# A hybrid S5 and gated DeltaNet block on one core: masks by selection, factored S5 tables, weight splits on VectorE, other figures in the planner of TensorE's order, an earlier first weight tile and five banks for the first transposes

## The chip, the cores and the metric

The kernel runs on one core of one Trainium2 chip. Time is device time in microseconds (us) of the slowest core, here the only one, and the median of three runs is given. Engines are named as in the profile: PE (TensorE), DVE (VectorE), ACT (ScalarE), POOL (GpSimd) and SP (SyncE, which here only issues transfers).

## The reference

One layer, 1024 tokens, 1024 channels, all float32. One projection of the normed input feeds two groups: a diagonal state-space group (S5, 32 groups of 16 channels, 64 states) and a gated DeltaNet group (4 heads of 128). A gate from per-token embeddings and a last norm follow.

In short:

```python
a = rms_norm(h, norm_mix_g[i])
proj = a @ w_in[i]                       # u_s, z_s, q, k, v, z_d, b_raw, a_raw
...
_, _, s_r, s_i = lax.associative_scan(_complex_linear_combine, (a_r, a_i, bu_r, bu_i), axis=1)
y = C_re s_r - C_im s_i + D * u_s; y = gelu(y); y_s = y * sigmoid(y @ w_glu + b_glu) * silu(z_s)
...
qkv = silu(causal_depthwise_conv(qkv, conv_w))          # 4 taps; q, k are L2-normed
g = -exp(A_log) * softplus(a_raw + dt_bias);  beta = sigmoid(b_raw)
g = cumsum(g) in chunks of 64;  decay = tril(exp(g_i - g_j))
sol = triangular_solve(tril(k_beta k^T * decay, -1) + I, [v_beta, k_beta * exp(g)])
per chunk: v_new = u - w S;  o = (q exp(g)) S + (q k^T * decay) v_new;  S = S exp(g_last) + k_dec^T v_new
y_d = rms_norm(o, norm_g) * silu(z_d)
h = h + concat(y_s, y_d) @ w_out
h = h + sigmoid(h @ w_gate) * rms_norm(p @ w_ple_proj, ple_norm_g)
return rms_norm(h, final_norm_g)
```

## The kernel before

**Products.** Float32 products are made of three (`mm3`, L117): each factor is split into a high part in the rounded type fp32r and the rest (`split`, L157: ACT writes the high part, another engine subtracts), and PE multiplies high by high, high by low and low by high. A weight tile (`wtile`, L581) is 128 input channels by 8 blocks of 128: one DMA into the only raw buffer (`wr`), an ACT copy into `wh`, a subtraction into `wl`, both with two buffers. The subtraction is on POOL, but for the tiles named in `EARLY` (L579), where VectorE makes it. `half` (L589) then makes one half of a tile's projection as 24 products of 128x512 into a bank named `pj`, 48 a tile.

**The start.** SP loads the embeddings and their weights, x in eight tiles, constants (`pk`, `wba`), then S5's small parameters (`hp`, and `ldt` in descriptors of single numbers), then the weight tiles, the first of which is number 20 of `win`. `e_proj` (L258) computes the embedding's projection meanwhile and its results are stored to `ed`. VectorE norms the tokens (`rms`, L193), and `scale_x` (L297) scales the eight x tiles. `xprep` (L287) transposes four x blocks into one bank `xtp`, from which ACT makes `ah` and VectorE `al`, the high and low parts of the normed input; eight blocks for the first half of the tokens (hf=0), eight for the second. `MM`, `MX` and `MZ` (L75 to L86) are pools of PE's banks with two or three banks each.

**The prefix scan of `a_raw`.** The decay logits are computed in an exact order of additions: `a_chain` (L1333) runs 64 steps; step n belongs to a group of eight, b = n // 8, and tells one half of the tokens, hf = b % 2. Each step has a part `a_prefix` (L696: three products of a bank `pT` with the masks `tg`; ACT moves it to a buffer F; VectorE subtracts neighbours; ACT makes two more columns) and, two steps on, `a_sums` (L717: four products with the masks `dg`, an ACT copy, four VectorE scans over F). In even groups an ACT copy takes the last column of the scans into `vst` (L730); in odd groups VectorE subtracts the last two columns into `se` (L728). Four buffers F go round. The masks `dg` and `tg`, one pair for each b, are made by `diag` (L327) as four POOL products for a group. The bank `pT` comes from the pool `MX`.

**S5.** `s5_params` (L354) makes the small coefficients and the powers `en` of the rotation by repeated squaring. For each of four batches `s5_batch` (L461) builds a table `tab` of 128 rotations by seven doublings of four POOL operations each (L514 to L525), scans, and puts the results out.

**The gates, the solve and the chunks.** `g_math` (L737) turns the sums in `se` into `gg`; PE transposes it (`gtp`), `decay` (L959) makes the masks, `subst` (L983) solves the 32 blocks on the diagonal, which needs VectorE's columns `cols`; `blocks` (L1045) and `double` (L1057) combine them on PE (`q`); `chunk` (L1171) then runs over the eight pairs of chunks, and `chunk_out` (L1226) norms and gates the result.

**The order.** PE's order is written by hand, by a planner at the end of the program (L1297 to L1469). It keeps a clock that counts only PE's work (`pec`, L104). Chains (`x_chain`, `a_chain`, `s5_chain`, `attn_chain`) yield the figure, from the table `LAT` (L449) or `PL` (L1321), that their next step has to wait; while no chain is due, PE is given the next piece of `fillers` (L1395): the projections in the order of the string `FILL`, then the rows of the glu gate (`pg`), the first half of the output projection (`out1`, L1126), and behind the chunks the rest (`out2`, `htrans`, `gate_out`, L1250). Larger figures so place more filler products ahead of a step. Other engines' orders come from the framework's scheduler, which goes by the program's order and by the inputs; every engine takes its queue in order.

Of the kernel before, what the change touches and what calls it, by code (L numbers as in the profile page):

```python
# [25 lines left out]
def hymba_block_kernel(ctx: ExitStack, tc: tile.TileContext, A: dict, out: bass.AP, dbg=None):  # L26
# [434 lines left out]
    def s5_batch(b):  # L461
# [54 lines left out]
        V.memset(tab[:, 0, :, 0:1], 1.0)  # L516
# [1007 lines left out]
```

## Time and profile before

| | us |
|---|---|
| median of the runs | 955.9 |
| the three runs | 954.72, 955.9, 956.91 |
| the profiled execution | 957.75 |
| its span | 956.0 |
| PE busy | 805.2 (84%) |
| weight loads busy | 649.1 (68%) |
| DVE busy | 709.2 (74%) |
| ACT busy | 489.6 (51%) |
| POOL busy | 343.4 (36%) |

The mean clock that PE was granted in that execution is 0.916 of full speed. The page's picture of the span in 40 equal slices (23.9 us each) shows the busy share of each engine in tenths, 9 for 90% or more, and PE's granted clock in the same way.

```profile
PE   6479889877798976988998597599579999899996
DVE  6946968988999878877548859953778754437886
ACT  7457667676696577766555244112355224113332
POOL 0120458676449348522102022101545219502222
PEclk9779989999899898998999798879789999999998
```

PE is nearly full in the last 170 us, and has slices of 40% and 50% at the start and near 520, 570 and 620 us, which the prediction looks at one by one. In rows of the timeline the first number is the start, the second the duration, and brackets give the idle time of the engine ahead of the instruction and what ended it.

### The profile page before, as it was taken

How to read it: one execution, taken by the hardware profiler on the slowest of the kernel's cores; microseconds unless marked ns; L12 is line 12 of the kernel's file. 1: busy time of each engine (PE TensorE's matmuls, PEld its weight loads, DVE VectorE, ACT ScalarE, POOL GpSimd, SP SyncE). 2: the span in 40 equal slices, each digit the busy share in tenths (PEclk: the TensorE clock that was granted, in tenths of full speed). 3: DMA queues.
4: the chain of work that ended last, by engine and by line, in shares of the span. 5: the costliest groups of instructions: out<-in, count | busy, mean ns of one | idle time of the engine just before them, and what ended most of it. 6: DMA issues, size and time to landing. Idle time of an engine off the chain costs nothing.

```text
span 956.0 us, 12315 instructions
## 1 busy us (share of the span) xinstructions
PE 805.2 (84%) x4338; PEld 649.1 (68%) x4338; DVE 709.2 (74%) x1478; ACT 489.6 (51%) x890; POOL 343.4 (36%) x326
## 2 busy tenths in 40 slices
PE   6479889877798976988998597599579999899996
PEld 3358468756686764876876376488467887778885
DVE  6946968988999878877548859953778754437886
ACT  7457667676696577766555244112355224113332
POOL 0120458676449348522102022101545219502222
PEclk9779989999899898998999798879789999999998
DMA  7430211403122031132102032104445534301211
GB/s 273 154 120 1 88 34 40 110 14 96 37 60 82 34 88 51 23 136 86 66 1 67 22 133 93 40 2 146 108 107 165 194 140 138 129 1 67 88 45 67
DMA packets 67581, 79.93 MB, mean 84 GB/s; under 512 B 23456, under 2 KB 49344, under 8 KB 67520
## 3 DMA queue, kind: packets, MB, share of 16 engines
q1 hardware_dynamic: 67376, 78.89, 25.9%
q8 instruction: 34, 0.56, 0.2%
q14 instruction: 27, 0.22, 0.1%
q10 hardware_dynamic: 144, 0.26, 0.1%
HBM read 57.39 MB, written 21.74 MB: 83 GB/s over the span
## 4 chain that ended last, share of the span: by engine, by line
PE 48%; DVE 27%; ACT 11%; issue 5%; DMA 5%; POOL 4%; SPq 1%; DVEq 0%; ACTq 0%; POOLq 0%
PE pj L111 16%; DVE F L726 9%; PE pq L111 9%; PE pT L111 6%; PE po L111 5%; ACT F L102 5%; DVE s5x L91 3%; PE bk L111 2%; DMA wr<-in_win 2%; DVE cv L99 2%; PE pg L111 2%; DVE pT L91 2%; ACT L102 1%; POOL wgl L91 1%; DVE s5x L554 1%
## 5 line engine op out<-in xcount | busy, mean ns | idle before, releaser
L111 PE MATMUL pj<-ah,wh 128*128 128x512 f32 x384 | 161.8, 421 | 12.3 <-ACT z L102 6.0
L111 PE MATMUL pj<-ah,wl 128*128 128x512 f32 x384 | 156.8, 408 | 0.7 <-POOL wl L91 0.7
L111 PE MATMUL pj<-al,wh 128*128 128x512 f32 x384 | 157.3, 410 | 0.0
L102 ACT ACTIVATE F<-F,gridc 128x512 f32<-128x512 f32 x128 | 115.2, 986 | 0.0
L91 POOL TENSOR_TENSOR wl<-wr,wh 128x1024 fp32r<-128x1024 f32 x21 | 52.2, 2485 | 137.6 <-ACT wh L102 137.6
L111 PEld LDWEIGHTS pj<-ah,wh 128*128 128x128 f32 x384 | 76.7, 200 | 31.9 <-ACT z L102 6.4
L111 PE MATMUL pT<-tg,ah 128*128 128x512 f32 x128 | 58.0, 453 | 47.0 <-ACT F L102 45.6
L726 DVE TENSOR_TENSOR_SCAN F<-F,vst 128x192 f32<-128x192 f32 x128 | 92.9, 784 | 3.2 <-ACT F L102 3.1
L726 DVE TENSOR_TENSOR_SCAN F<-F 128x192 f32<-128x192 f32 x128 | 85.7, 729 | 7.2 <-ACT F L102 7.1
L111 PEld LDWEIGHTS pj<-ah,wl 128*128 128x128 f32 x384 | 75.9, 198 | 19.5 <-POOL wl L91 1.2
L111 PEld LDWEIGHTS pj<-al,wh 128*128 128x128 f32 x384 | 76.4, 199 | 16.4
L91 DVE TENSOR_TENSOR pT<-F 128x512 f32<-128x512 f32 x64 | 51.0, 797 | 47.9 <-ACT F L102 46.4
L111 PEld LDWEIGHTS pT<-tg,ah 128*128 128x128 f32 x128 | 26.3, 205 | 60.7 <-ACT F L102 51.1
L111 PE MATMUL pq<-wgl,hth 128*128 128x512 f32 (+1 forms) x200 | 66.9, 386 | 0.0
L102 ACT ACTIVATE F<-pT 128x512 f32<-128x512 f32 x64 | 55.5, 867 | 2.1 <-PE pT L111 2.1
L99 DVE SCALAR_TENSOR_TENSOR cv<-raw,pk,cv 128x1023 f32<-128x1023 f32 (+2 forms) x36 | 52.9, 1470 | 3.9 <-ACT cv L102 3.8
L91 POOL TENSOR_TENSOR e<-e,pleg 128x1024 f32<-128x1024 f32 x8 | 19.3, 2412 | 97.7 <-ACT jq L102 88.3
L91 DVE TENSOR_TENSOR h<-h,po 128x512 f32<-128x512 f32 x32 | 21.9, 686 | 40.9 <-PE po L111 40.8
L102 ACT ACTIVATE F<-pT,tbl 128x128 f32<-128x128 f32 x128 | 36.5, 372 | 28.4 <-PE pT L111 28.3
L706 POOL COPY F<-tbl 128x4 f32<-128x4 f32 x32 | 16.5, 517 | 84.5 <-DVE pT L91 84.5
L102 ACT ACTIVATE wh<-wr 128x1024 fp32r<-128x1024 f32 x24 | 25.3, 1052 | 37.9 <-DMA wr<-in_win 14.9
L111 PE MATMUL pT<-dg,al 128*128 128x512 f32 x128 | 44.2, 429 | 0.0
(337 smaller groups left out, 2033.5 us busy)
## 6 DMA issues: line engine op xcount, KB each, us to landing
wr<-in_win SPq DMA_DIRECT2D x24, 512.0 KB, 3.7
x<-in_x SPq DMA_DIRECT2D x8, 512.0 KB, 8.1
wr<-in_wout SPq DMA_DIRECT2D x8, 512.0 KB, 4.0
h<-in_x SPq DMA_DIRECT2D x8, 512.0 KB, 4.6
wr<-in_wgate SPq DMA_DIRECT2D x8, 512.0 KB, 3.3
e<-ed SPq DMA_DIRECT2D x8, 512.0 KB, 3.2
out<-h SPq DMA_DIRECT2D x7, 512.0 KB, 2.6
ed<-e SPq DMA_DIRECT2D x6, 512.0 KB, 12.6
```

Of the source, the lines that this page charges most:

```text
L91: return e.tensor_tensor(out=o, in0=a, in1=b, op=op)
L99: return e.scalar_tensor_tensor(out=o, in0=a, scalar=s, in1=b, op0=op0, op1=op1)
L102: return S.activation(out=o, in_=i, func=f, **k)
L111: return PE.matmul(o, lhsT=l, rhs=r, start=a, stop=z, **k)
L554: V.tensor_tensor_scan(out=flat(w[:, ri]), data0=flat(rh), data1=flat(v[:, ri]), initial=0.0, op0=MUL, op1=ADD)
L706: G.tensor_copy(out=tb[:, :, 0:1], in_=first)
L726: V.tensor_tensor_scan(out=d0, data0=d0, data1=d1, initial=vst[:, i, h:h + 1] if hf else 0.0, op0=ADD, op1=ADD)
```

## The change

- **First weights:** the DMA of weight tile 20 is issued right behind `wba`, ahead of S5's `hp` and `ldt`, and `wtile` takes it from there.
- **Banks at the start:** `e_proj` and the first half's `xprep` take two of five banks from `MX`, the others from their old pool; `x_chain` yields 0 in the first half, where it yielded 1.2.
- **x:** `scale_x` is one tile at a time; tiles 0 to 3 are scaled as before, tiles 4 to 7 between the first four `xprep`. The split of weight tile 21 is held until tile 0 is scaled.
- **Splits:** every weight tile's `wl` is subtracted on VectorE; the list `EARLY` goes.
- **Selections:** the masks of a group are two `affine_select`s on POOL of 128x1024 instead of four products of 128x512.
- **Tables:** `s5_params` builds two small tables once for all batches (16 and 8 rotations, in the new tile `rt4`, by `rotate`, four and three doublings of four POOL operations), and `s5_batch` makes `tab` as their product: eight POOL products of 2x8x16 elements and two operations of 512.
- **`se`:** odd groups copy the last two columns on ACT into `se2`, as even groups copy `vst`; one subtraction in `g_math` makes `se` of them, in a buffer F.
- **Planner:** six figures in `LAT` and three in `PL`.
- **Smaller:** `rr`, `v2` and `tq` of `chunk` live in `rt4`; the scratch tiles of `rsqrt` with 32 columns and more have one buffer.

```diff
-        p = MM("pe")
+        p = (MX if i % 5 % 2 else MM)("pe")
...
+    wfirst = {20: raw_w([P, 8, P])}
+    SP.dma_start(out=wfirst[20], in_=A["win"][20].rearrange("p (k c) -> p k c", k=8))
...
-        p = MZ("xtp", [P, 4, P])
+        p = (MX if hf == 0 and k % 5 % 2 else MZ)("xtp", [P, 4, P])
...
-    def scale_x():
-        for i in range(8):
-            r = ts(V, xt_[i], xt_[i], rinvs[:, i:i + 1], MUL)
-        return r
+    sx = {}
+
+    def scale_x(i):
+        sx[i] = ts(V, xt_[i], xt_[i], rinvs[:, i:i + 1], MUL)
...
-    scale_x()
+    for i in range(4):
+        scale_x(i)
...
-    se = C("se", [P, 4, 8, 4])
+    se2 = C("se2", [P, 4, 8, 4, 2])
...
+    wap = C("wap", [P, 8, 2, 4], F32R)
+    V.tensor_copy(out=wap[:, :, 0], in_=wba[:, :, 4:8])
+    tt(V, wap[:, :, 1], wba[:, :, 4:8], wap[:, :, 0].bitcast(F32), SUB)
...
-        for x, w in enumerate((wah.bitcast(F32), wal)):
-            for o, m in zip(res, (ident, tri)):
-                tt(G, o[:, x], w[:, b, :].unsqueeze(2).to_broadcast(sh), m.unsqueeze(1).to_broadcast(sh), MUL)
+        w = wap[:, b].rearrange("p x h -> p (x h)").unsqueeze(2).to_broadcast([P, 8, P])
+        for o, c in zip(res, (ALU.is_equal, ALU.is_ge)):
+            G.affine_select(out=o.rearrange("p x h c -> p (x h) c"), in_=w, pattern=[[0, 8], [1, P]],
+                            compare_op=c, fill=0.0, base=0, channel_multiplier=-1)
...
+    rt4 = C("rt4", [P, 8, P])
+    rtf = rt4.rearrange("p a b -> p (a b)")
+    tbs = [rtf[:, a:z].rearrange("p (r j n) -> p r j n", r=2, j=16) for a, z in ((0, 512), (512, 768))]
+    tbx = rtf[:, 768:1024].rearrange("p (r j n) -> p r j n", r=2, j=16)
+
+    def rotate(tb, x, i, c, s):
+        n = 1 << i
+        tt(G, tb[:, :, :, n:2 * n], tb[:, :, :, 0:n], c, MUL)
+        tt(G, x[:, :, :, 0:n], tb[:, :, :, 0:n], s, MUL)
+        tt(G, tb[:, 0, :, n:2 * n], tb[:, 0, :, n:2 * n], x[:, 1, :, 0:n], SUB)
+        tt(G, tb[:, 1, :, n:2 * n], tb[:, 1, :, n:2 * n], x[:, 0, :, 0:n], ADD)
...
+        for tb, e0, n in ((tbs[0], 0, 4), (tbs[1], 4, 3)):
+            V.memset(tb[:, 0, :, 0:1], 1.0)
+            V.memset(tb[:, 1, :, 0:1], 0.0)
+            for i in range(n):
+                c0, s0 = (e.unsqueeze(1).unsqueeze(3).to_broadcast([P, 2, 16, 1 << i]) for e in en[e0 + i])
+                rotate(tb, tbx, i, c0, s0)
...
-        prep=14.1, ev=3.3, scan=18.0, tab=8.7, g1=13.5, g2=10.6, dec=14.8, sub=14.7, blk=0.3,
-        q32=6.9, d32=6.5, q64=2.0, d64=0.8, kq=4.3, A=1.4, B=4.8, C=1.4, otp=10.3, vtp=23.2, ssq=30.3,
+        prep=14.1, ev=3.3, scan=18.0, tab=6.0, g1=23.0, g2=4.0, dec=14.8, sub=25.0, blk=0.3,
+        q32=6.9, d32=8.0, q64=2.0, d64=0.8, kq=4.3, A=1.4, B=4.8, C=1.4, otp=10.3, vtp=23.2, ssq=30.3,
...
-        V.memset(tab[:, 0, :, 0:1], 1.0)
-        V.memset(tab[:, 1, :, 0:1], 0.0)
-        for i in range(7):
-            n = 1 << i
-            cc = en[i][0][:, pp].unsqueeze(1).unsqueeze(3).to_broadcast([P, 2, 4, n])
-            ss = en[i][1][:, pp].unsqueeze(1).unsqueeze(3).to_broadcast([P, 2, 4, n])
-            tt(G, tab[:, :, :, n:2 * n], tab[:, :, :, 0:n], cc, MUL)
-            tt(G, tb[:, :, :, 0:n], tab[:, :, :, 0:n], ss, MUL)
-            tt(G, tab[:, 0, :, n:2 * n], tab[:, 0, :, n:2 * n], tb[:, 1, :, 0:n], SUB)
-            tt(G, tab[:, 1, :, n:2 * n], tab[:, 1, :, n:2 * n], tb[:, 0, :, 0:n], ADD)
+        t5, x5 = (t.rearrange("p r j (m n) -> p (r j) m n", n=16) for t in (tab, tb))
+        for j in range(4):
+            lo = tbs[0][:, :, 4 * b + j].unsqueeze(2).to_broadcast([P, 2, 8, 16])
+            ch, sh_ = (tbs[1][:, r, 4 * b + j].unsqueeze(1).unsqueeze(3).to_broadcast([P, 2, 8, 16]) for r in range(2))
+            tt(G, t5[:, j:8:4], lo, ch, MUL)
+            tt(G, x5[:, j:8:4], lo, sh_, MUL)
+        tt(G, tab[:, 0], tab[:, 0], tb[:, 1], SUB)
+        tt(G, tab[:, 1], tab[:, 1], tb[:, 0], ADD)
...
-    EARLY = (12, 13, 16)
-
...
-        raw = raw_w([P, 8, P])
-        SP.dma_start(out=raw, in_=A["win"][mt].rearrange("p (k c) -> p k c", k=8))
-        split(hi, lo, raw, S, V if mt in EARLY else G)
+        raw = wfirst.pop(mt, None)
+        if raw is None:
+            raw = raw_w([P, 8, P])
+            SP.dma_start(out=raw, in_=A["win"][mt].rearrange("p (k c) -> p k c", k=8))
+        with ExitStack() as st:
+            if mt == 21:
+                gate(st, sx[0])
+            split(hi, lo, raw, S, V)
...
-            tt(V, se[:, b // 2, i, :], f[:, 382:1536:384], f[:, 383:1536:384], SUB)
+            act(se2[:, b // 2, i], f[:, 0:1536].rearrange("p (h c) -> p h c", h=4)[:, :, 382:384], AF.Copy)
...
+        se = FT[0][:, 0:128].rearrange("p (a b c) -> p a b c", a=4, b=8)
+        tt(V, se, se2[:, :, :, :, 0], se2[:, :, :, :, 1], SUB)
...
-        f0=8.0, x1=26.0, a0=23.9, ca=5.2, s0=34.0, x0=16.7,
+        f0=8.0, x1=20.5, a0=20.5, ca=5.2, s0=30.0, x0=16.7,
...
-            yield LAT["xp"]
+            if hf == 0 and k < 4:
+                scale_x(4 + k)
+            yield LAT["xp"] if hf else 0
```

SP's queue at the start, behind the eight loads of x; `ed<-e` stores the embedding's projection, `wr<-in_win` loads a weight tile. Before:

```order
L281 DMA pk<-in_pk 128x134
L282 DMA wba<-in_wba 128x64
L340 DMA hb_413<-in_hp 128x8
L343 DMA ldt<-in_ldt 64x16x1 x2
L585 DMA wr<-in_win 128x1024
L274 DMA ed<-e 128x1024 x5
L268 DMA ed<-e 128x512
L585 DMA wr<-in_win 128x1024
L268 DMA ed<-e 128x512 x3
```

With the change:

```order
L281 DMA pk<-in_pk 128x134
L282 DMA wba<-in_wba 128x64
L284 DMA wr<-in_win 128x1024
L343 DMA hb_410<-in_hp 128x8
L346 DMA ldt<-in_ldt 64x16x1 x2
L274 DMA ed<-e 128x1024 x5
L268 DMA ed<-e 128x512 x2
L603 DMA wr<-in_win 128x1024
L268 DMA ed<-e 128x512 x2
```

The first weight tile stands ahead of `hp` and `ldt`; the second, behind five stores of 128x1024 and one of 128x512 before, now stands behind five and two.

ACT's queue in the last steps of an odd group (F and its number are the four buffers that go round, `raw`, `cv` and `z` evacuate projections, `wh` is the split of a weight tile). Before:

```order
L102 ACTIVATE F_406<-pT,tbl 128x128 x4
L102 ACTIVATE F_408<-pT 128x512
L102 ACTIVATE F_406<-F_406,gridc 128x512 x2
L102 ACTIVATE raw<-pj 128x512
L102 ACTIVATE cv<-pj,pk 128x512
L102 ACTIVATE F_407<-pT,tbl 128x128 x4
L102 ACTIVATE F_405<-pT 128x512
L102 ACTIVATE F_407<-F_407,gridc 128x512 x2
L102 ACTIVATE wh<-wr 128x1024
L102 ACTIVATE raw<-pj 128x512
L102 ACTIVATE cv<-pj,pk 128x512
```

With the change, where `se_399` is the tile `se2`:

```order
L102 ACTIVATE se_399<-F_403 128x8
L102 ACTIVATE F_406<-pT,tbl 128x128 x4
L102 ACTIVATE F_404<-pT 128x512
L102 ACTIVATE F_406<-F_406,gridc 128x512 x2
L102 ACTIVATE raw<-pj 128x512
L102 ACTIVATE cv<-pj,pk 128x512
L102 ACTIVATE se_399<-F_404 128x8
L102 ACTIVATE F_403<-pT,tbl 128x128 x4
L102 ACTIVATE F_405<-pT 128x512
L102 ACTIVATE F_403<-F_403,gridc 128x512 x2
```

Each odd step now has one copy that reads F behind the scans, and the moves of `pT` to F of later steps stand behind it in the queue.

PE's queue around the first products `q` of the solve (`pj` is a projection, `kq` the attention scores of k and q, `pg` the glu gate). Before:

```order
L111 MATMUL pj<-ah_139,wh 128x512
L111 MATMUL pj<-al_147,wh 128x512
L111 MATMUL pj<-ah_139,wl 128x512
L111 MATMUL q_4656<-q_4289,zt_3646 32x32 x16
L111 MATMUL q_4656<-q_4289,zt_3691 32x32 x16
L111 MATMUL q_4691<-q_4289,zt_3704 32x32 x16
L111 MATMUL q_4691<-q_4289,zt_3739 32x32 x16
L111 MATMUL kq<-q_4289,k_3640 128x128 x4
L111 MATMUL pj<-ah_140,wh 128x512
L111 MATMUL pj<-al_148,wh 128x512
```

With the change:

```order
L111 MATMUL pj<-al_152,wh 128x512
L111 MATMUL pj<-ah_144,wl 128x512
L111 MATMUL kq<-em_4331,k_3516 128x128 x4
L111 MATMUL kq<-q_4345,k_3518 128x128 x8
L111 MATMUL q_4702<-q_4345,zt_3524 32x32 x16
L111 MATMUL q_4702<-q_4345,zt_3537 32x32 x16
L111 MATMUL q_4737<-q_4345,zt_3570 32x32 x16
L111 MATMUL q_4737<-q_4345,zt_3583 32x32 x16
L111 MATMUL kq<-q_4359,k_3520 128x128 x4
L111 MATMUL pg<-gh_4796,wgh 128x512
L111 MATMUL pg<-gl_4795,wgh 128x512
```

The `q` products stood among projections of the fillers; now the last projection is ahead of them, with eight more `kq`, and the glu gate's products follow. Counted from PE's first instruction, 1071 projection products stood ahead of the first `q` before, and all 1152 do now. Between the last `pT` product of the prefix scan and `gtp` the queue had 54 projection products and has 144; between `gtp` and the transposes `pe` that follow, it had 48 and has 18.

In chunk 6 and the front of chunk 7 PE's queue holds no products of the output projection between those of the chunk itself; before, both had them.

More of the change, by code (lines that the diff above doesn't have):

```diff
@@ L130, in rsqrt @@
         n = "rs" + "x".join(map(str, shp[1:]))
-        hb = dp.tile(shp, I32, tag=n + "h", name="hb")
-        t = dp.tile(shp, F32, tag=n + "t", name="rt")
+        hb = dp.tile(shp, I32, tag=n + "h", name="hb", bufs=3 if shp[1] < 32 else 1)
+        t = dp.tile(shp, F32, tag=n + "t", name="rt", bufs=3 if shp[1] < 32 else 1)
         V.tensor_scalar(out=hb, in0=x.bitcast(I32), scalar1=1, scalar2=None, op0=ALU.logical_shift_right)
@@ L322, in hymba_block_kernel @@
     FT = [fp.tile([P, FW], F32, tag="F", name=f"F{i}") for i in range(4)]
-    wah, wal = C("wah", [P, 8, 4], F32R), C("wal", [P, 8, 4])
-    V.tensor_copy(out=wah, in_=wba[:, :, 4:8])
-    tt(V, wal, wba[:, :, 4:8], wah.bitcast(F32), SUB)
+    wap = C("wap", [P, 8, 2, 4], F32R)
+    V.tensor_copy(out=wap[:, :, 0], in_=wba[:, :, 4:8])
+    tt(V, wap[:, :, 1], wba[:, :, 4:8], wap[:, :, 0].bitcast(F32), SUB)
     def diag(b):
-        sh = [P, 4, P]
         res = [T(f"{n}{b}", F32R, [P, 2, 4, P]) for n in ("dg", "tg")]
-        for x, w in enumerate((wah.bitcast(F32), wal)):
-            for o, m in zip(res, (ident, tri)):
-                tt(G, o[:, x], w[:, b, :].unsqueeze(2).to_broadcast(sh), m.unsqueeze(1).to_broadcast(sh), MUL)
+        w = wap[:, b].rearrange("p x h -> p (x h)").unsqueeze(2).to_broadcast([P, 8, P])
+        for o, c in zip(res, (ALU.is_equal, ALU.is_ge)):
+            G.affine_select(out=o.rearrange("p x h c -> p (x h) c"), in_=w, pattern=[[0, 8], [1, P]],
+                            compare_op=c, fill=0.0, base=0, channel_multiplier=-1)
         return res
@@ L1191, in chunk @@
                 mm(bk[:, 2, :], ksl(qq, n, h), Sst[h])
-                rr = dp.tile([P, P], F32, tag="rr", name="rr", bufs=4)
+                rr = rt4[:, h]
                 stt(V, rr, bk[:, 0, :], neg[:, ucs[h]], vr[c][:, i, h, :], MUL, ADD)
-                tq = dp.tile([P, P], F32, tag="tq", name="tq", bufs=4)
+                tq = rt4[:, 4 + h]
                 act(tq, bk[:, 2, :], AF.Copy, scale=eg[:, ucs[h]])
@@ L1202, in chunk @@
             mm(bks[h][:, 1, :], zu(4 * n + h), rrs[h])
-            v2 = rrs[h] if n else dp.tile([P, P], F32, tag="rr", name="v2", bufs=4)
+            v2 = rrs[h] if n else rt4[:, h]
             ts(V, v2, bks[h][:, 1, :], dd[:, ucs[h]], MUL)
```

## Prediction

> **What bounds the kernel now.** I read the stretch table first, cut where the kind of work changes. Columns: busy time (instructions) of PE, weight loads, DVE, ACT, POOL, then the granted clock, DMA share and GB/s.
>
> ```profile
> 0.00:67.00 67.00, 40.02 (x140) 27.96 (x140) 46.43 (x93) 39.01 (x47) 8.70 (x14) 0.86 0.55 195
> 67.00:520.00 453.00, 392.03 (x2012) 312.30 (x2012) 364.88 (x586) 309.56 (x542) 214.50 (x248) 0.93 0.20 58
> 520.00:622.00 102.00, 72.22 (x317) 57.29 (x319) 83.86 (x211) 31.14 (x45) 17.06 (x10) 0.85 0.21 73
> 622.00:786.00 164.00, 143.90 (x1146) 122.58 (x1143) 107.56 (x285) 55.09 (x136) 49.22 (x29) 0.90 0.40 123
> 786.00:956.00 170.00, 157.06 (x733) 128.97 (x732) 106.49 (x306) 54.83 (x122) 53.93 (x26) 0.97 0.22 78
> ```
>
> PE's idle time is what can be won: 27 us before the first prefix product, 61 in the prefix-scan stage (to 520), 30 in the gate chain (to 622), 20 among the chunks, 13 behind them. The wait table (total, times, longest) names the largest cause.
>
> ```profile
> PE pT L111 <- ACT F L102: 45.6, 17, 6.9
> ACT vst L102 <- DVE F L726: 55.7, 21, 5.3
> ```
>
> The scan stage loses PE time through ACT, which itself stands behind VectorE's scans. The gate chain (rows further down) loses it because the planned PE order reaches gtp and q before VectorE has their input.
>
> **The start.** Timeline rows (start, duration; in brackets the idle time before).
>
> ```profile
> ldt<-in_ldt SPq DMA_DIRECT2D x2, 4.0 KB, 18.5
> 20.00:31.00 11.00, 7.39 (x28) 4.48 (x27) 10.89 (x16) 10.87 (x10) 0.00 (x0) 1.00 0.07 4
> 31.00:40.00 9.00, 1.60 (x6) 0.97 (x6) 7.94 (x39) 0.00 (x0) 0.00 (x0) 0.86 0.33 120
> 40.00:50.00 10.00, 7.08 (x21) 5.67 (x22) 8.79 (x17) 3.67 (x6) 2.70 (x1) 0.61 0.84 324
> 41.32 1.06 ACT L102 ACTIVATE wh<-wr 128x1024 fp32r<-128x1024 f32 x1 [10.45 <-DMA wr<-in_win]
> 41.52 7.51 DVE L95 TENSOR_SCALAR x<-x,rsc 128x1024 f32<-128x1024 f32 x8
> 53.72 1.26 ACT L102 ACTIVATE ah<-xtp,pk 128x512 fp32r<-128x512 f32 x2
> 62.76 2.08 PE L115 MATMUL xtp<-cm,x 128*128 128x128 f32 x8 [0.66 <-DVE al L99]
> 69.13 0.80 PE L111 MATMUL pT<-tg,ah 128*128 128x512 f32 x1 [0.78 <-POOL tg L91]
> ```
>
> The first weight tile queues behind ldt, 4 KB that take 18.5 us while the queue moves 4 GB/s, and holds ACT 10.45 us. Ahead of ldt it costs nothing there. What is late next? VectorE finishes the norm at 41.5 as before, plus one split put into it (1.2), then scales four x tiles instead of eight: 3.75, so 46.5. But SP now queues the second weight tile behind seven stores of e (3.07 MB), and ACT and VectorE split it ahead of the first ah and of x4 to x7. About 1.08 MB of the 3.6 move by 40 (9 us at 120 GB/s), the rest needs 2.5 MB / 324 GB/s = 7.7 us: it lands near 48, so the first ah runs at 49 instead of 53.72, minus 4.7. The banks save some 2 us more over the eight pairs (the 0.6 to 2 us waits on al); POOL's two selects come behind the last first-half transpose as its four products did. **Start: minus 7**, from minus 2 (tile at 52) to minus 10 (tile no obstacle).
>
> **The scan stage.** VectorE and POOL first.
>
> ```profile
> L91 POOL TENSOR_TENSOR wl<-wr,wh 128x1024 fp32r<-128x1024 f32 x21 | 52.2, 2485 | 137.6 <-ACT wh L102 137.6
> L91 DVE TENSOR_TENSOR wl<-wr,wh 128x1024 fp32r<-128x1024 f32 x3 | 3.6, 1216 | 10.1 <-ACT wh L102 10.1
> L91 DVE TENSOR_TENSOR se<-F 128x4 f32<-128x4 f32 x32 | 10.5, 328 | 0.5
> L726 DVE TENSOR_TENSOR_SCAN F<-F,vst 128x192 f32<-128x192 f32 x128 | 92.9, 784 | 3.2 <-ACT F L102 3.1
> L726 DVE TENSOR_TENSOR_SCAN F<-F 128x192 f32<-128x192 f32 x128 | 85.7, 729 | 7.2 <-ACT F L102 7.1
> 231.94 1.90 DVE L726 TENSOR_TENSOR_SCAN F<-F 128x192 f32<-128x192 f32 x4
> 238.00 4.00 DVE L726 TENSOR_TENSOR_SCAN F<-F 128x192 f32<-128x192 f32 x4
> 237.49 3.65 POOL L91 TENSOR_TENSOR s5x<-s5x,s5x 128x512 f32<-128x512 f32 x2 [5.01 <-DVE ssq L882]
> 248.76 0.55 DVE L726 TENSOR_TENSOR_SCAN F<-F 128x192 f32<-128x192 f32 x1
> 67.00:520.00 453.00, 20.06 (x32) 67.41 (x112) 0.93 0.20 58
> 67.00:520.00 453.00, 77.04 (x256) 53.39 (x256) 19.15 (x15) 0.93 0.20 58
> L970 POOL TENSOR_SCALAR_AFFINE_SELECT em<-em 128x1024 f32<-128x1024 f32 x3 | 5.0, 1678 | 28.8 <-DVE em L91 28.8
> ```
>
> Four scans take 1.90 us with POOL quiet and 4.00 beside a POOL product; against 0.55 for one alone the two groups carry 128 x 0.234 + 128 x 0.179 = 53 us of excess, 0.25 us for each of POOL's 214.5 in this stage. The GPSIMD Engine Reference of the Trainium skill (Key points) says that GpSimd shares its SBUF interfaces with VectorE and contends with instructions that have two SBUF inputs; the trace agrees, 4.00 against 1.90. By the same rule the moved splits, which read two SBUF inputs, would be stretched too; that is a rival below.
>
> The two stretch rows are those of the table's tile (VectorE's work, then POOL's x112) and of the mask dg (PE, weight loads, then POOL's x15; tg has as much); the last row is an affine select. POOL loses 15 splits (15 x 2.485 = 37). Per batch the tables become eight products of 256 columns and two of 512; at the 1.83 us that one 512-wide product takes above (3.65 for two), and half of that for 256, that is 11 a batch or 44, and 28 small operations once, which the 112 small and large ones put below 0.6 each, 15: 59 for 67. The masks become 14 selects at 1.68, 24 for 38. In all minus 60, so minus 15 of scan excess. VectorE gains 15 x 1.216 = 18 and gives up 10.5 with se. Net minus 7. VectorE is busy in 81% of this stage's 453 us, so I count **minus 6**.
>
> What ACT does in return is the dangerous part.
>
> ```profile
> 252.73 0.21 ACT L102 ACTIVATE vst<-F 128x4 f32<-128x4 f32 x1 [6.11 <-DVE s5tab L516]
> 254.78 0.79 PE L111 MATMUL pT<-tg,ah 128*128 128x512 f32 x1 [6.01 <-ACT F L102]
> ```
>
> A copy of 0.21 us waits 6.11 for VectorE's scans (the row names the memset that stands right behind them); behind it in ACT's queue stand the evacuations that free PE's bank, and PE stands 6.01. So far only the even groups of eight steps have such a copy (vst); the odd ones took se on VectorE, free of any wait on ACT. Now every step has one. Ends for the stage: plus 25 (half of what even steps lose, 45.6, on the odd ones too), and minus 30 (POOL's relief halves the 45.6, VectorE's 7 on top). I take minus 6, nearest to the VectorE rows.
>
> **The gate chain.**
>
> ```profile
> 547.59 0.19 DVE L91 TENSOR_TENSOR gg<-F 128x32 f32<-128x32 f32 x1
> 547.84 0.40 PE L115 MATMUL gtp<-cm,gg 128*32 128x128 f32 x1 [10.78 <-DVE gg L91]
> 550.94 0.21 DVE L849 COPY F<-gls 32x128 f32<-32x128 f32 x1
> 561.50 0.49 PE L115 MATMUL pe<-cm,F 32*128 32x32 f32 x5
> 561.11 1.23 DVE L91 TENSOR_TENSOR wl<-wr,wh 128x1024 fp32r<-128x1024 f32 x1 [9.96 <-ACT wh L102]
> 621.57 3.63 PE L111 MATMUL q<-q,zt 32*32 32x32 f32 x128 [10.70 <-DVE q L1048]
> 507.10 4.19 PE pj L111 x18
> 760.99 1.79 PE bk L111 x16
> 774.88 1.78 PE bk L111 x16
> 683.82 0.80 PE L111 MATMUL pg<-gh,wgh 128*128 128x512 f32 x1 [4.09 <-ACT gh L102]
> ```
>
> A projection product costs 4.19 / 18 = 0.233 us. PE now has 144 of them between the last prefix and gtp where it had 54: 90 x 0.233 = 21 more than the 10.78 that it stands there, so gtp comes up to 10 later than gg, less what VectorE's g_math slips meanwhile: the last v tiles' convolutions now fall ahead of gtp, not behind it. I take 2 late. Between gtp and pe stand 18 products, before 48: VectorE's last row is ready at 551.15, PE reached pe at 561.50, and would now at 552.4: minus 9. **To the first q: minus 7.** Ends: 0 (VectorE stands at wl until ACT's split comes, 9.96 here, so cols is no earlier) and minus 12.
>
> **Behind q.** PE reaches q with 1152 projections done, before 1071: 81 x 0.233 = 18.9 us of work that no longer follows. The 4.09 before pg and the waits like it go (its inputs load while PE waits for q): minus 6. Against it stands a new empty place: the order has no filler in chunk 6 and the front of chunk 7, where out1 is used up and out2 has not begun. A chunk takes 13.9 us (760.99 to 774.88), 39 x 0.233 = 9.1 of them filler. If its chain needs all of that time, the 1.4 chunks idle 13 us, if only PE limits it, none; I take 7. **Minus 18**, ends minus 6 (13 idle) and minus 25 (none).
>
> What else moves I cost at nothing. e's products over five banks: they end under VectorE's norm, which closes at 41.5 whatever PE does; without that cover PE's 27 idle us of the start would move with them. rr and tq in one tile: the same eight blocks of a chunk. The smaller rsqrt buffers: nothing waits for them in these rows.
>
> **The sum.** The profiled execution took 957.75 us, span 956.0; the median of the runs is 955.9, and I carry the difference over to it: 955.9 - 7 - 6 - 7 - 18 = **918**.
>
> **The rivals.**
> - *The copies hold the scans up.* The odd steps lose on ACT what the even ones lose now, 45.6 us, and POOL's relief is used up by the splits: 955.9 - 7 - 7 - 18 + 45.6 = 970, slower. It decides from 32 us on, 1.0 us in each of the 32 odd steps. For it: vst waits 55.7 us in 21 of 32 steps with the same neighbours in the queue. Against it: the wait exists because scans run at 4.00 and not at 1.90, and POOL has 60 us less to disturb them with.
> - *The stage gets all the relief.* Minus 30 there: 894. For it: 45.6 us of PE waiting in 17 places, behind contended scans; against it, VectorE's work hardly falls.
> - *The time is given back later.* Gate chain 0, behind q minus 6: 955.9 - 7 - 6 - 6 = 937. For it: the unfilled chunks, and VectorE's 9.96 in front of cols; against it: PE is 97% granted and over 90% busy from 786 on, so work done before q is work saved.
> - *The splits meet POOL.* POOL stays busy in some 154 of the 453 us, a third; a third of the splits' 18 us would take twice as long, as the scans do: stage 0, 955.9 - 32 = 924. For it the two scan rows, against it the three splits that VectorE does already, mean 1.216 with no stretch to see. (The GPSIMD Engine Reference of the Trainium skill, Key points, gives the ground for it.)
> - *The early load does nothing*, since the second tile holds what the first one held (it lands at 52 or later): start 0, 955.9 - 31 = 925.
>
> **Chances.** Forecast 0.36, full relief 0.20, given back 0.18, splits 0.06, second tile 0.06, coupling 0.14, of which 0.03 end within 0.2% (about what a measurement of this kernel can tell from no change) and 0.11 slower. Faster 0.86. The range goes from 892, just under the full relief's 894, to 948, beyond the given-back case and half way into the coupling; about 0.15 is left out.
>
> **What would show it.** Start: ACT's first split has no wait for wr, the first ah at 49, the first prefix complete near 62; wrong if ACT waits for the second wr beyond 50. Stage: POOL's busy time down by about 60, the mean scan near 0.65 us, the last scan group near 507; wrong if ACT's waits for scans (vst and se2 together) exceed 90 us and PE's wait on ACT grows from 45.6. Gate chain: gtp without a wait, pe within 6 us of it, the first q near 602. Behind it: pg among the d products, one idle place of 5 to 10 us before the last chunk. The prediction falls if the stage from the first prefix to the last scan takes over 480 us.

## The result, and the profile after

The changed kernel takes 929.12 us (median of 4 runs, 927.48 to 930.28) where the kernel before takes 955.72; the ratio is 0.972, with a 95% interval of 0.9701 to 0.9739. The forecast was 918 in a range of 892 to 948: the sign was right, and 27 us came of the 38. The profiled execution took 930.28 us, with a span of 928.6.

| us from the start | before | after | forecast |
|---|---|---|---|
| first `ah` | 53.7 | 49.3 | 49 |
| first prefix product complete | 69.9 | 61.7 | 62 |
| last group of scans ends | 523.8 | 517.4 | 507 (by the terms of its sum 511) |
| `gtp` starts | 547.8 | 552.2 | gg + 2 |
| first `q` | 621.6 | 621.8 | 602 |
| from there to the end | 334.4 | 306.8 | 316 |

So the kernel is 8 us ahead after the start, 6 after the scans, nothing at the first `q`, and 27 at the end. The stretch table of after has the columns of the first one of before (busy time of PE, weight loads, DVE, ACT, POOL, then granted clock, DMA share, GB/s), with the same cuts.

```profile
0.00:67.00 67.00, 41.62 (x168) 31.89 (x169) 47.84 (x97) 41.44 (x52) 4.07 (x13) 0.90 0.54 195
67.00:520.00 453.00, 396.93 (x2039) 313.50 (x2038) 355.93 (x583) 313.20 (x574) 141.98 (x171) 0.93 0.19 58
520.00:622.00 102.00, 75.25 (x353) 60.04 (x353) 85.08 (x197) 36.13 (x48) 20.67 (x12) 0.90 0.36 112
622.00:786.00 164.00, 147.10 (x1176) 126.77 (x1173) 115.21 (x309) 60.02 (x149) 55.22 (x32) 0.92 0.41 126
786.00:928.60 142.60, 129.84 (x613) 106.91 (x611) 94.01 (x281) 41.94 (x103) 33.82 (x17) 0.96 0.16 60
```

POOL fell by 73 us in the scan stage (the forecast had about 60), VectorE by 9, and PE's idle time there only from 61 to 56. The two stretches from the first `q` to the end, before and after, have the same columns.

```profile
621.60:956.00 334.40, 301.36 (x1885) 251.95 (x1885) 214.43 (x592) 110.30 (x259) 103.15 (x55) 0.93 0.31 100
```

```profile
621.80:928.60 306.80, 277.13 (x1788) 233.87 (x1788) 209.41 (x590) 102.16 (x251) 89.04 (x49) 0.94 0.29 95
```

Behind the first `q` PE's busy time fell by 24.2 and its idle time by 3.4: the gain that is left at the end lies there. The wait table of after shows what replaced the old waits.

```profile
ACT vst L102 <- DVE F L747: 50.0, 21, 5.6
...
ACT se L102 <- DVE F L747: 42.4, 23, 5.7
...
PE pT L111 <- ACT F L102: 28.9, 22, 4.5
...
PE q L111 <- DVE q L1071: 20.3, 1, 20.3
```

PE's wait on ACT fell from 45.6 to 28.9, although ACT now waits 92 us for scans (50.0 and 42.4), and PE's wait for `q` doubled to 20.3. The start, in rows of the timeline:

```profile
31.04 1.14 ACT L102 ACTIVATE wh<-wr 128x1024 fp32r<-128x1024 f32 x1
...
48.38 1.06 ACT L102 ACTIVATE wh<-wr 128x1024 fp32r<-128x1024 f32 x1 [10.73 <-DMA wr<-in_win]
49.34 2.40 ACT L102 ACTIVATE ah<-xtp,pk 128x512 fp32r<-128x512 f32 x4
```

```profile
60.75 0.50 PE L111 MATMUL pT<-tg,ah 128*128 128x512 f32 x1 [1.24 <-POOL tg L334]
```

The first split runs at 31.04 without a wait; the second tile holds ACT until 48.38, and the first `ah` follows at 49.34.

### The profile page after: what moved, and what is told of

Read it like the earlier page. It is cut to its first block, busy times and chain, and to the rows that moved or that the text cites. A ratio compares the mean times of both kernels' runs of the same rounds, so it can differ in the third digit from the quotient of the medians.

```text
span 928.6 us, 12239 instructions
## 1 busy us (share of the span) xinstructions
PE 790.8 (85%) x4338; PEld 639.1 (69%) x4338; DVE 698.1 (75%) x1464; ACT 492.7 (53%) x922; POOL 255.8 (28%) x245
## 4 chain that ended last, share of the span: by engine, by line
PE 44%; DVE 30%; ACT 12%; DMA 5%; issue 4%; SPq 2%; POOL 2%; DVEq 0%; ACTq 0%; POOLq 0%
PE pj L111 12%; PE pq L111 10%; DVE F L747 8%; PE po L111 7%; ACT F L102 5%; PE pT L111 5%; PE bk L111 3%; DVE s5x L91 3%; DVE q L91 2%; PE pg L111 2%; DVE pT L91 2%; DVE sq L188 2%; ACT L102 2%; DVE cv L99 2%; DVE xt L91 1%
## 5 line engine op out<-in xcount | busy, mean ns | idle before, releaser
L111 PE MATMUL pj<-ah,wh 128*128 128x512 f32 x384 | 159.5, 415 | 15.2 <-DVE ssq L905 8.6
L111 PE MATMUL pj<-al,wh 128*128 128x512 f32 x384 | 155.1, 404 | 0.0
L747 DVE TENSOR_TENSOR_SCAN F<-F 128x192 f32<-128x192 f32 x128 | 79.8, 681 | 14.6 <-ACT F L102 14.5
L111 PEld LDWEIGHTS pj<-al,wh 128*128 128x128 f32 x384 | 75.5, 197 | 16.3
L747 DVE TENSOR_TENSOR_SCAN F<-F,vst 128x192 f32<-128x192 f32 x128 | 80.0, 686 | 8.0 <-ACT F L102 7.7
L111 PE MATMUL pT<-tg,ah 128*128 128x512 f32 x128 | 56.9, 444 | 33.8 <-ACT F L102 28.9
L727 POOL COPY F<-gridc 128x4 f32<-128x4 f32 x32 | 13.6, 425 | 161.0 <-DVE pT L91 91.9
L99 DVE SCALAR_TENSOR_TENSOR cv<-raw,pk,cv 128x1023 f32<-128x1023 f32 (+2 forms) x36 | 50.7, 1408 | 0.1
L111 PE MATMUL pT<-dg,ah 128*128 128x512 f32 x128 | 42.9, 418 | 0.0
L111 PEld LDWEIGHTS pq<-wgl,hth 128*128 128x128 f32 x200 | 37.1, 188 | 7.4
```

Of the source, the lines that this page charges most:

```text
L99: return e.scalar_tensor_tensor(out=o, in0=a, scalar=s, in1=b, op0=op0, op1=op1)
L111: return PE.matmul(o, lhsT=l, rhs=r, start=a, stop=z, **k)
L727: G.tensor_copy(out=tb[:, :, 0:1], in_=first)
L747: V.tensor_tensor_scan(out=d0, data0=d0, data1=d1, initial=vst[:, i, h:h + 1] if hf else 0.0, op0=ADD, op1=ADD)
```

## The experiments

Twelve kernels were run. Differences are between medians; the kernel before had 955.8 to 956.3 beside them. Rows come from one profiled execution each. The last group of scans, whose work no edit of e8 and e10 touches, ends at 519.5 and 517.9 there and at 517.4 in the changed kernel, so that the end of a stage is good to some 2 us.

### The planner's figures and the rest, apart

e1 puts the nine new figures alone into the kernel before; e2 makes the same edit the other way round in the changed kernel.

```diff
-        prep=14.1, ev=3.3, scan=18.0, tab=8.7, g1=13.5, g2=10.6, dec=14.8, sub=14.7, blk=0.3,
-        q32=6.9, d32=6.5, ...
+        prep=14.1, ev=3.3, scan=18.0, tab=6.0, g1=23.0, g2=4.0, dec=14.8, sub=25.0, blk=0.3,
+        q32=6.9, d32=8.0, ...
-        f0=8.0, x1=26.0, a0=23.9, ca=5.2, s0=34.0, x0=16.7,
+        f0=8.0, x1=20.5, a0=20.5, ca=5.2, s0=30.0, x0=16.7,
```

> The kernel before with only the planner's nine new figures. Theory A (the forecast's sum): the gate chain's 7 and the 18 behind the first q come from the order alone, so 955.9 - 25 = 931. Theory B (the order pulls all projections ahead of the first q, but fills 10 us too many in front of gtp and brings POOL's work for the glu gate beside the substitution): the first q comes 7 to 10 later than 621.6 and the stretch behind it 27 shorter, so 936 to 939.

> The changed kernel with the nine old figures of the planner. Theory A: start and scan stage keep their 13, so 943, the first q near 608. Theory B: gg is 6 earlier as in the changed kernel, no more comes from the scan stage, gtp follows gg at once and the first q comes near 615, with nothing gained behind it: 948 to 950.

e1 took 950.35 (10 runs, ratio 0.9955, 0.9934 to 0.9975), e2 935.91 (0.9808, 0.9775 to 0.9841). Both theories missed both times, though A's first `q` of e2 is met (608.2). In e1's profile (span 954.0) the first `q` comes at 646.7, 25 later than before, and from there to the end it takes 307.3, 27 less: the saving behind `q` is a matter of the figures alone, and so is a loss of nearly the same size ahead of it. (This execution was the slowest of the ten, 5 above the median, so the loss may be that much too large here.) In e2 (span 933.5) the last scans end at 517.8, as with the new figures, the first `q` comes 13 earlier than before, and 9 more are saved behind it (325.4 for 334.4). So the edits on the engines are worth 20 without the new figures, and the new figures 6 to 7 either way, not the forecast's 25. Of e1's loss the last scans show 23 already (546.8 for 523.8); `gg` is 18 late, and `gtp` 35:

```profile
565.95 0.19 DVE L91 TENSOR_TENSOR gg<-F 128x32 f32<-128x32 f32 x1
...
582.48 0.27 PE L115 MATMUL gtp<-cm,gg 128*32 128x128 f32 x1
```

It starts 16.3 behind the end of `gg` (566.1), because PE is still in the projections that the figures put ahead of it.

### The first weight tile, and the banks

e3 moves only the first weight tile's transfer, in the kernel before:

```diff
     SP.dma_start(out=wba, in_=A["wba"])
+    wfirst = {20: raw_w([P, 8, P])}
+    SP.dma_start(out=wfirst[20], in_=A["win"][20].rearrange("p (k c) -> p k c", k=8))
```

> The kernel before with only the first weight tile's transfer moved ahead of hp and ldt. Theory A: the first ah at 49 and the end 4 to 5 earlier, 951. Rival: the gain is used up in the scan stage, where ACT and VectorE wait for each other whenever it begins; first ah at 49 all the same, the last scan within 2 of 523.7 and the end at 954 to 957.

It took 951.37 (10 runs, 0.9952, 0.9927 to 0.9978): 5 faster, as theory A has it. The first `ah` is at 48.6, the last scans end at 518.9 instead of 523.8, so the gain passes through the scan stage whole.

e12 gives the changed kernel its old pools of banks:

```diff
-        p = (MX if i % 5 % 2 else MM)("pe")
+        p = MM("pe")
...
-        p = (MX if hf == 0 and k % 5 % 2 else MZ)("xtp", [P, 4, P])
+        p = MZ("xtp", [P, 4, P])
```

> The changed kernel with the old pools of banks for the embedding's products and the first half's transposes. Theory A: the first prefix product 2 us later, 61.7 to 64, and the end 2 later, 931. Rival: the transposes wait for VectorE's x, not for banks; nothing moves, 928 to 930.

It took 933.51 (931.13 to 934.97): the first prefix product is complete at 64.1 instead of 61.7, as theory A has it, and the end comes 4 later, where it had 2.

### How full the place ahead of gtp is

The changed kernel's own rows, from `gg` to the first `q`:

```profile
541.34 0.19 DVE L91 TENSOR_TENSOR gg<-F 128x32 f32<-128x32 f32 x1
...
552.18 0.28 PE L115 MATMUL gtp<-cm,gg 128*32 128x128 f32 x1
...
555.16 0.22 DVE L872 COPY F<-gls 32x128 f32<-32x128 f32 x1
...
556.57 0.38 PEld L115 LDWEIGHTS pe<-cm,F 32*128 32x128 f32 x5 [0.37 <-issue]
```

`gg` is done at 541.53 and `gtp` starts 10.6 later. e4 puts one figure back:

```diff
-        prep=14.1, ev=3.3, scan=18.0, tab=6.0, g1=23.0, g2=4.0, dec=14.8, sub=25.0, blk=0.3,
+        prep=14.1, ev=3.3, scan=18.0, tab=6.0, g1=13.5, g2=4.0, dec=14.8, sub=25.0, blk=0.3,
```

> The changed kernel with the one figure g1 back at 13.5, which leaves 105 projection products between the last pT and gtp instead of 144. Theory A (gtp was forecast 2 us late): at most 2 us, 927. Theory B (the trace has gtp 10.6 us behind gg): 39 x 0.233 = 9 us earlier at pe and at the first q, and 920 at the end. If the projections that now stand behind gtp delay what VectorE needs there, less, down to no gain.

It took 921.7 (919.83 to 923.54, ratio 0.9652): 7.4 faster than the changed kernel, near theory B's 920. Its rows:

```profile
540.52 0.19 DVE L91 TENSOR_TENSOR gg<-F 128x32 f32<-128x32 f32 x1
...
540.91 0.27 PE L115 MATMUL gtp<-cm,gg 128*32 128x128 f32 x1
...
546.71 0.38 PEld L115 LDWEIGHTS pe<-cm,F 32*128 32x128 f32 x5 [0.17 <-issue]
```

`gtp` now follows `gg` at once, `pe` comes 9.9 earlier, and the first `q` 14.4 earlier, at 607.5. The 4.5 beyond the 9.9 come from the next point, mainly: the substitution takes 30.6 here for 36.6. Of the 14.4, 7.3 are given back behind `q`, in the chunks (125.1 from the first to the last `bk`, the bank of a chunk's own products, for 116.7), where 18 more products of the glu gate stand.

### Who stands beside the substitution

From the end of the preparing memset to the transposes behind it, `subst` takes VectorE 29.6 us before and 36.6 after; its 62 operations take 23.7 and 32.5. In e2 and e11, where POOL does none of its large products beside them, they take 21.2. The rows of after (POOL and VectorE; `wgl` and `gl` are splits for the glu gate):

```profile
599.24 2.49 POOL L91 TENSOR_TENSOR wgl<-wgr,wgh 128x1024 fp32r<-128x1024 f32 x1 [4.55 <-ACT wgh L102]
599.45 0.68 DVE L91 TENSOR_TENSOR em<-kq,em 128x512 f32<-128x512 f32 x1
...
600.05 1.95 DVE L91 TENSOR_TENSOR q<-q,xt 128x240 f32<-128x240 f32 x1
...
606.00 5.90 POOL L91 TENSOR_TENSOR gl<-gr,gh 128x1024 fp32r<-128x1024 f32 x2 [4.27 <-ACT gh L102]
606.30 2.90 DVE L91 TENSOR_TENSOR xt<-q,q 128x175 f32<-128x175 f32 x1
...
609.23 2.87 DVE L91 TENSOR_TENSOR q<-q,xt 128x175 f32<-128x175 f32 x1
...
612.13 0.32 DVE L91 TENSOR_TENSOR xt<-q,q 128x156 f32<-128x156 f32 x1
```

While POOL makes `gl`, an operation of 0.34 us (its time in e10, below) takes 2.90 and the next 2.87; the one at 612.13, when POOL is done, takes 0.32. Under `wgl` the operation at 600.05 takes 1.95, and the one at 599.45, which reads `kq` from PSUM, its usual 0.68. With the projections used up early, the splits of the glu gate come up beside the substitution. e8 moves them, and the products `zs` of the gate, to VectorE:

```diff
-                split(wgh[i], wgl[i], raw)
+                split(wgh[i], wgl[i], raw, S, V)
...
-            split(v8(hi), v8(lo), raw.rearrange("p b j c -> p b c j"))
+            split(v8(hi), v8(lo), raw.rearrange("p b j c -> p b c j"), S, V)
...
-            tt(G, z.rearrange("p (c j) -> p c j", j=8), z.rearrange("p (c j) -> p c j", j=8),
+            tt(V, z.rearrange("p (c j) -> p c j", j=8), z.rearrange("p (c j) -> p c j", j=8),
```

> The changed kernel with the glu gate's splits and products (wgl, gl, zs) on VectorE instead of POOL, where they ran beside the substitution. Theory B: the 62 operations of the substitution take 22 to 24 us as in the other runs instead of 32.5, of which VectorE gives back 2.4 to 6 for the work it takes over; first q at 614 to 617, end 923 to 925. Rival (the substitution is long for another reason): operations stay near 32 and the end comes 2 to 6 later than 929.

It took 930.76 (929.79 to 933.45). The 62 operations are back at 21.2 us, a little below theory B's 22 to 24, but VectorE itself now spends 11.0 on other work there instead of 2.8 (`gl` takes 1.9 each, `zs` 1.0), so the first `q` stays at 622.7 and theory B's 923 to 925 is missed: the cause is shown, the cure is none. e10 holds POOL's `gl` and `zs` instead, behind a small copy on POOL that reads the result:

```diff
             tt(V, xx[:, 0:k, k:32], xx[:, 0:k, k:32], tm, SUB)
+        sbl.append(G.tensor_copy(out=sscr, in_=flat(xx)[:, 31:32]))
...
+            gate(st, *aft)
             return tt(e2, lo, raw, hi.bitcast(F32), SUB)
```

> The changed kernel with POOL's splits gl and products zs of the glu gate held until the substitution is done (a copy of one column of its result on POOL stands ahead of them), wgl as it was. Theory B (it is POOL's work beside the substitution that stretches it): the 62 operations take 25 us instead of 32.5, the first q comes at 615, and since pg then waits some 3 us for gl, the end comes at 923 to 926. Rival (the time is given back as PE waits for gl and zs): first q at 615 all the same, end at 928 to 931.

It took 925.3 (920.03 to 926.14), 3.8 faster. The 62 operations take 24.4, the first `q` comes at 615.6, the end at 924.4 in the profile: theory B, though the wait of 3 that it had for `pg` isn't there (1.6, as in the changed kernel). Its rows:

```profile
601.41 2.44 POOL L91 TENSOR_TENSOR wgl<-wgr,wgh 128x1024 fp32r<-128x1024 f32 x1 [4.59 <-ACT wgh L102]
601.57 0.68 DVE L91 TENSOR_TENSOR z<-kq,z 128x512 f32<-128x512 f32 x1
...
602.17 1.94 DVE L91 TENSOR_TENSOR xt<-q,q 128x231 f32<-128x231 f32 x1
...
604.63 0.38 DVE L91 TENSOR_TENSOR q<-q,xt 128x231 f32<-128x231 f32 x1
...
607.49 0.34 DVE L91 TENSOR_TENSOR xt<-q,q 128x175 f32<-128x175 f32 x1
...
611.80 0.19 POOL L1022 COPY sscr<-q 128x1 f32<-128x1 f32 x1 [7.95 <-DVE q L91]
611.94 2.89 POOL L91 TENSOR_TENSOR gl<-gr,gh 128x1024 fp32r<-128x1024 f32 x1
```

`wgl`, which was left where it was, still holds one operation (602.17, 1.94 us), and `gl` starts behind the last one. The operation of 128x175 at 607.49 is the one that took 2.90 above.

### The parts of the scan stage

e5 takes `se` on VectorE again; e6 has the old tables and the old masks; e7 puts the splits back on POOL in the changed kernel; e11 puts all of them on VectorE in the kernel before.

```diff
-            act(se2[:, b // 2, i], f[:, 0:1536].rearrange("p (h c) -> p h c", h=4)[:, :, 382:384], AF.Copy)
+            tt(V, se[:, b // 2, i, :], f[:, 382:1536:384], f[:, 383:1536:384], SUB)
```

> The changed kernel with se taken by VectorE again (32 subtractions of 0.33 us), without the copies on ACT. Theory A (the forecast counted these as pure VectorE time): 10.5 x 0.81 = 8 slower, 937. Rival (coupling: the copies wait 42 us for scans on ACT and hold the moves of pT behind them, as much as they save): 925 to 930, with PE's wait on ACT down from 28.9.

e5 took 923.02 (917.63 to 926.72), 6.1 faster than the changed kernel and 2 below the rival's 925 to 930. The last scans end at 511.0 instead of 517.4, and PE's wait on ACT is down to 23.4 from 28.9. The copies cost 6, net of the VectorE time that they save, and that is less than was counted: the 32 subtractions take 6.3 here, where they took 10.5 before.

```diff
-        t5, x5 = (t.rearrange("p r j (m n) -> p (r j) m n", n=16) for t in (tab, tb))
...
+        for i in range(7):
+            n = 1 << i
+            tt(G, tab[:, :, :, n:2 * n], tab[:, :, :, 0:n], cc, MUL)
...
-            G.affine_select(out=o.rearrange("p x h c -> p (x h) c"), in_=w, pattern=[[0, 8], [1, P]],
+                tt(G, o[:, x], w[:, b, :].unsqueeze(2).to_broadcast(sh), m.unsqueeze(1).to_broadcast(sh), MUL)
```

> The changed kernel with the old tables of S5 (seven doublings on POOL in each batch) and the old masks (four POOL products a group). Theory A: POOL gets back 8 + 14 = 22 us, VectorE's scans a quarter of that, 5.5, times 0.81: 4 to 5 slower, 933.5. Theory B (POOL's work counts more than by the scans, since PE also waits for tables and masks, 8 us in the run with the figures alone): 8 to 15 slower, 937 to 944.

e6 took 942.79 (938.63 to 943.01), 13.7 slower (its profiled execution 8): theory B. VectorE's busy time in the stage rises by only 4 (360.2 for 356.0) for 42 more of POOL, 0.1 us for each, but PE now waits for POOL and the tables (3.6 for `tg` in the changed kernel's stage, and not for the others):

```profile
PE pT L111 <- POOL tg L91: 6.0, 3, 3.5
...
PE pj L111 <- DVE s5tab L536: 5.1, 1, 5.1
PE yps L111 <- POOL s5x L91: 4.7, 2, 3.9
```

```diff
-            split(hi, lo, raw, S, V)
+            split(hi, lo, raw, S, V if mt in (12, 13, 16) else G)
```

> The changed kernel with the subtractions of the weight tiles on POOL again, but for the old three. Theory A: POOL busy 37 more and scans 9 longer, VectorE 18 freed: 7 faster in the stage, 922. Theory B (each split beside a scan group stretches both, and POOL is late with wl for PE): no gain or slower, 929 to 938.

> The kernel before with all splits of the weight tiles on VectorE, nothing else. Theory A (the forecast's terms: 18 more on VectorE, 37 less on POOL and so 9 less in the scans): 7 slower, 963. Theory C (a split on POOL costs more than the scans show: it stretches whatever VectorE does, and comes late for PE; undone in the changed kernel it cost 15 to 22): 8 to 15 faster, 941 to 948. If the splits matter only together with the new order of PE: within 3 of 956.

e7 took 951.08 (10 runs, 945.93 to 956.83), 22 slower than the changed kernel, and 16 by the two profiled executions, from which the rows are; e11 took 946.37 (0.9917, 0.9888 to 0.9945), 9 faster than before, although its first prefix product comes 6.8 late (VectorE's first split, at 42.18, waits 8.2 for ACT's `wh`, with the rest of the norm behind it). The forecast's terms had the other sign in both; e7's theory B had the sign, but 929 to 938 was too little, and e11's theory C holds. The rows of e7 are VectorE's busy time from the first prefix to the last scan, then that of the tile `wl` alone (PE, weight loads, VectorE, POOL), each followed by the granted clock, the DMA share and GB/s:

```profile
58.50:530.90 472.40, 364.22 (x561) 0.91 0.18 55
```

```profile
58.50:530.90 472.40, 116.07 (x287) 55.87 (x287) 2.44 (x2) 38.01 (x15) 0.91 0.18 55
```

And of the changed kernel (VectorE; then PE, weight loads, VectorE):

```profile
61.70:517.40 455.70, 355.95 (x576) 0.93 0.19 57
```

```profile
61.70:517.40 455.70, 116.19 (x285) 56.03 (x286) 22.20 (x17) 0.93 0.19 57
```

Apart from `wl` VectorE is busy 364.22 - 2.44 = 361.8 us in e7 and 355.95 - 22.20 = 333.8 in the changed kernel: 15 splits on POOL, 38.0 us, stretch everything else on VectorE by 28.0, 0.74 us for each of theirs. Between the kernel before and e11 it is the same 28.0 (367.9 - 2.4 against 359.7 - 22.2). The scans explain a quarter of it in the first pair (0.713 us each in e7, 0.682 after, 256 scans, 8 us) and 16 us in the second.

### Both edits that helped

e9 is the changed kernel with the edits of e4 and e5:

```diff
-        prep=14.1, ev=3.3, scan=18.0, tab=6.0, g1=23.0, g2=4.0, dec=14.8, sub=25.0, blk=0.3,
+        prep=14.1, ev=3.3, scan=18.0, tab=6.0, g1=13.5, g2=4.0, dec=14.8, sub=25.0, blk=0.3,
...
-            act(se2[:, b // 2, i], f[:, 0:1536].rearrange("p (h c) -> p h c", h=4)[:, :, 382:384], AF.Copy)
+            tt(V, se[:, b // 2, i, :], f[:, 382:1536:384], f[:, 383:1536:384], SUB)
```

> The changed kernel with both edits that made it faster: se taken by VectorE again (923.0 in its run) and g1 at 13.5 (921.7). If the two act in different places (the copies on ACT in the scan stage, the filling ahead of gtp in the gate chain), their gains of 6 and 7 add: 915 to 917. If both only move the same slack, 920 to 922.

It took 911.76 (6 runs, 908.24 to 916.89; 0.9561, 0.9535 to 0.9587): 44 faster than before and 17 faster than the changed kernel. The gains add, and a little more. The stretches, cut at its first prefix product, last scan, first `q` and last chunk, columns as above:

```profile
0.00:61.90 61.90, 38.13 (x139) 28.58 (x140) 45.65 (x94) 37.49 (x45) 3.86 (x12) 0.89 0.58 211
61.90:505.20 443.30, 394.34 (x2058) 316.29 (x2057) 360.85 (x608) 311.88 (x546) 143.71 (x172) 0.93 0.20 60
505.20:597.50 92.30, 79.10 (x355) 63.67 (x353) 76.13 (x203) 34.66 (x48) 8.64 (x7) 0.93 0.29 98
597.50:760.10 162.60, 144.78 (x1153) 122.95 (x1154) 122.79 (x295) 60.00 (x140) 66.60 (x36) 0.91 0.44 136
760.10:906.50 146.40, 133.25 (x637) 109.70 (x635) 101.78 (x298) 46.31 (x114) 35.01 (x18) 0.99 0.17 61
```

The scan stage is 12 shorter than that of the changed kernel (443.3 for 455.7), of which e5 and e4 had shown 6.5 and 1.6 (the latter within what two executions differ by), and so is the gate chain (92.3 for 104.4).

## Why the prediction was right in sign and 11 short

By stages the forecast had minus 7, 6, 7 and 18, and the profiles show minus 8.2, plus 1.8, plus 6.6 and minus 27.6. That the sum came within 11 is in part luck: two terms had the wrong sign, 21 in all, and a gain behind `q` that was 10 larger hid half of it.

**Start, minus 7: right.** Measured 8.2, and by its own steps: the second tile lands near 48 (48.38), first `ah` at 49 (49.34), some 5 for the early tile (e3), 2 for the banks (64.1 to 61.7 in e12).

**Scan stage, minus 6: wrong, plus 2** (453.9 to 455.7 from the first prefix to the last scan). Three of its steps failed. "0.25 us for each of POOL's 214.5" was read from the scans alone, and as one price for all of POOL's work; for the tables and masks it is 0.1 (e6), for the splits 0.74, three times that, so that the splits, counted at 18 on VectorE for 9 of relief, in fact free VectorE of 28 for 20 of work; alone they shorten the stage from 453.9 to 436.9 (e11, where it starts 6.8 later). And "gives up 10.5 with se" was counted as a gain, where the copies cost 6 (e5): the mechanism of the coupling rival, at a fifth of the 1.0 us a step from which it would have decided. The forecast left the planner's figures out of this stage, though in the kernel before they lengthen it by 19 (first prefix at 74.0, last scan at 546.8 in e1). The third is the step from VectorE's work to the stage: between the same two events VectorE's busy time fell by 11.9 (367.9 to 356.0), more than the forecast's net 7, and the stage took no less. Nor does PE's work alone set its length here: with the new figures 30 more projections stand in it (856 for 826) and it takes 455.7, with the old ones (e2) there are 817 and it takes 454.8. What stays open is the sum: early tile 5, splits 10 to 13.5, tables and masks 9, copies minus 6, each measured at the end of the last scan beside one state or another of the rest, make 18 or more, and all together have 6, with the old figures as with the new. PE's order is fixed, and what one edit frees another may already have freed; no run tells which.

**Gate chain, minus 7: wrong, plus 6.6** (97.8 to 104.4 from the last scan to the first `q`). "I take 2 late" for `gtp` was the failed step: it rested on VectorE slipping among the convolutions of the last v tiles, but `gg` followed the last scan as before (24.1 us for 24.0), 6.3 earlier than before, and `gtp` came 10.6 behind it, the upper end that the text itself had worked out. e4 shows the price, 9.9 at `pe`. The step from `gtp` to `pe`, minus 9, held: 13.7 became 4.4. The second failure was an omission: the forecast named the 81 projections pulled ahead of `q` and not what follows them in the queues, the glu gate's work on POOL. It stretches the 62 operations of the substitution by 8.8 and the substitution by 7.0, and e10 takes 8.1 off the operations.

**Behind q, minus 18: right in mechanism, 27.6 in size.** The 81 projections (18.9 at 0.233) are gone from there: busy time falls by 24.2, and 16 products `kq` and the clock (0.94 for 0.93) can make up most of the rest. They are not all saved, as the forecast had it: 3 now stand in the start, 30 in the scan stage and 48 in the gate chain, where PE's idle time fell by only 5.5 and 1.6. The waits among the chunks, put at 6, were more: between the first and the last product `bk` PE idled 18.5 and idles 12.7, of which 7 are new. The unfilled place, put at 7, is there as forecast, in chunk 6. The rows are PE's (busy time, granted clock, DMA share, GB/s) in the filled chunk before and in the unfilled one after:

```profile
760.80:774.80 14.00, 14.00 (x86) 1.00 0.42 141
```

```profile
753.00:767.10 14.10, 7.82 (x43) 0.68 0.40 130
```

A chunk takes 14.1 us with 43 products as it took 14.0 with 86, and PE idles 6.3 of it at a lower granted clock.

**The rivals.** "The time is given back later" put the gate chain at 0 and the stretch behind it at minus 6, and was wrong in both. "The stage gets all the relief", minus 30 there, is refuted by the stage's plus 2. "The copies hold the scans up" is the cost of the copies above, far too small to make the kernel slower. "The splits meet POOL" is right in kind and too large: of the 24 splits on VectorE two are held (1.75 and 2.23 us, the others 1.22), 1.5 us in all, where it had 6. "The early load does nothing" is refuted by e3.

## What to carry to other kernels

Price a helper engine's work by what it does to all that the other engine does beside it, for each kind of work apart, read from that engine's whole busy time, and not from one kind of instruction. A figure that lets a planner put more work ahead of a late step has two prices, the step's lateness once the wait is filled, and whatever queues up next when that work is used up early; look up on every engine what that is and what stands beside it. After engines have been relieved, set such figures again: here one of them, put back, was worth 7 us.

## What the hardware did that was not expected

In these rows VectorE does not slow down beside POOL, it stops. An operation that reads two SBUF tiles and takes 0.34 us took 2.90, and ended just behind POOL's instruction (at 609.20; the first of POOL's two runs from 606.00 to 609.00). Operations that read one operand from PSUM pass: in e10 `z<-kq,z` runs at 601.57 in its usual 0.68 us under the same POOL instruction that holds the next operation for 1.94. The page "SBUF — State Buffer" of the Trainium skill (SBUF: two separate sides) states this, an exclusive lock on a shared pair of ports, which whoever starts first keeps for the whole instruction, between VectorE operations with two SBUF inputs and POOL instructions that read SBUF. The rows agree. They also show POOL held in its turn: before, a product `dg` that starts at 242.80 beside a VectorE scan (241.92 to 243.92) takes 1.95 us, where the shortest take 1.04. So what a POOL instruction costs VectorE depends on what stands beside it; why the 42 us of tables and masks in e6 cost it no more than 4 is not shown.

The other surprise is PE's clock. The engine line of the page of after:

```profile
PE 790.8 (85%) x4338; PEld 639.1 (69%) x4338; DVE 698.1 (75%) x1464; ACT 492.7 (53%) x922; POOL 255.8 (28%) x245
```

The same 4338 products kept PE busy 790.8 us for 805.2 before, at a mean granted clock of 0.928 for 0.916. So 14 of the 27 us are less busy time for the same products and 13 less idling. As an estimate from these two clocks, 805.2 x (1 - 0.916 / 0.928) = 10.4 of the 14 are the clock's. Its scatter is smaller than the difference: the changed kernel's four executions have 0.921 to 0.932, those of the kernel before, run beside e4, 0.906 to 0.919. What sets it stays open; e4, which idles 17 us less than the changed kernel, has 0.924 to 0.933, no clear difference.
